# A mixture-of-experts tail with 26 units in place of 28: the largest experts in three strips of 32 slots, each beside a small expert

## The chip, the cores and the metric

The kernel runs on one core of a Trainium2 chip. A core has five engines: TensorE (PE, with its weight loads shown as PEld), VectorE (DVE), ScalarE (ACT), GpSimd (POOL) and SyncE (SP, here the engine that issues nearly all loads). Sixteen DMA engines move data between HBM and the on-chip SBUF. The metric is the device time of one execution in microseconds (us), the median over several runs.

## The reference

Two blocks run one after the other on 256 tokens of width 1024: a transformer block with two feed-forward layers, and a second block that ends in a mixture of experts. Only the end of the second block is touched here. In outline:

```
scores = sigmoid(h @ w_router)                  # 256 tokens x 64 experts
sel = scores + b_router; keep the best 4 of 8 groups of experts
top_e = top_k(sel, 8)                           # each token goes to 8 experts
w = scores[top_e] / sum * 2.5
for each expert e, on its own tokens:
    gate, up = split(h[tok] @ w_gu[e])          # w_gu[e]: 1024 x 512
    acc[tok] += w * ((silu(gate) * up) @ w_down[e])   # w_down[e]: 256 x 1024
y = acc + shared expert(h)                      # one expert that sees every token
out = x + gt2 * rms_norm(y)
```

All is float32. The experts' weights are 6144 numbers on each of 128 partitions, 3 MB for one expert and 192 MB for 64. Every expert's weights are read once. Counted from the reference for the given inputs, the 2048 pairs of token and expert spread unevenly: the largest expert has 73 tokens, the fifth largest 56, and the smallest 28 of the first 58 have 29 or fewer.

## The kernel before

Everything up to the router is the same instruction for instruction in both kernels and is left out here.

**Units.** The experts run in units of 128 slots. A slot is a place for one token of one expert. `UNITS` (line 33) is the order of the units, one letter each: F, two experts fixed by their number (the last eight, `NFIX`, "given" because no routing result is needed to know which they are); M, two experts of up to 64 tokens; H, one expert of up to 128 tokens; S, four experts of up to 32 tokens. Which experts take the places of H, M and S is found on the chip: `placement` (line 1616) ranks the first 56 experts by their count of tokens, so that the 4 largest fall to H, the next 28 to M, the rest to S. A list `plan` (line 1644) holds the expert's number for every place. Experts whose tokens don't fit would go through a loop at line 1911 that runs as often as needed; by the counts above it runs no time in either kernel.

**What a unit does on TensorE.** For each pair of units `gather` (L1792) picks the tokens' rows by a product with a one-hot matrix. Then, for each unit: `front` (L1809) multiplies the 128 slots by the gate and up weights in eight steps of 128 rows; each expert takes its own columns of the array (two of 64, one of 128, four of 32), and the first four steps read the expert's first tile, the last four its second. `back` (L1824 to L1846) transposes the activation, multiplies it by the down weights (L1841, the expert's third tile), scales by the routing weight on ACT and DVE. `scatter` (L1853) adds the result to the tokens' accumulators; it is issued one unit later, between the next unit's front and back.

**What orders the loads.** SP issues all expert loads (L1735) from one queue, in the order of the units, in tiles of 1 MB: in a unit first all first tiles, then all second, then all third, so an S unit has 12, F and M 6, H 3. There are 19 buffers (`NEX` + `NEX2`), used in turn: a load waits until TensorE has done the last product with the tile 19 places earlier. The numbers of a unit's experts are read from `plan` into SP's registers just ahead of that unit's loads (`entry`, L1741); the given experts need no such read. So SP can run ahead of TensorE by up to 19 tiles, but stops at the first planned unit until `plan` is written. In this text e1 to e192 are the expert tiles in the order of their loads; e1 to e24 belong to the four F units.

**Side work.** In the first units TensorE, DVE and ACT also do the shared expert, `placement` and `overflow`, in pieces between the expert products.

Of the kernel before, what the change touches and what calls it, by code (L numbers as in the profile page):

```python
# [13 lines left out]
ALU = mybir.AluOpType  # L14
# [6 lines left out]
T = 256  # L21
# [4 lines left out]
N_EX = 64  # L26
# [4 lines left out]
NFIX = 8  # L31
UNITS = "FFFFSSMHMSMMHMSMMHMSMMMHSMMM"
ROOM = {"F": (2, 64), "H": (1, 128), "M": (2, 64), "S": (4, 32)}
# [3 lines left out]
def column_plan():  # L37


    count = {k: UNITS.count(k) * ROOM[k][0] for k in "HMS"}  # L40
    assert sum(count.values()) == N_EX - NFIX and 2 * UNITS[:NFIX // 2].count("F") == NFIX
    at = {"H": 0, "M": count["H"], "S": count["H"] + count["M"]}
    cols, first = [], []
    for k in UNITS[NFIX // 2:]:
        first.append(len(cols))
        for _ in range(ROOM[k][0]):
            cols.extend((at[k], s) for s in range(0, ROOM[k][1], 64))
            at[k] += 1
    return cols, first, count["H"], count["H"] + count["M"]


COLS, FIRST_COL, RANK_M, RANK_S = column_plan()
NCOL = len(COLS)

# [94 lines left out]
class Kern:  # L149
# [55 lines left out]
    def root(self, v, b, n):  # L205

        nc = self.nc
        r = self.small([128, 1], "r", 12)
        nc.scalar.activation(r, v, AF.Sqrt, scale=1.0 / n, bias=b)  # L209
        nc.vector.reciprocal(r, r)  # L210
        return r
# [691 lines left out]
    def second_ffn(self, p):  # L903
# [11 lines left out]
        def load_x():  # L915
            for c in range(2):
                nc.gpsimd.dma_start(out=cx[:, c, :], in_=A["ctx"][128 * c:128 * c + 128, :])
            self.lower = self.small([128, 128], "lower", 1)
            nc.gpsimd.dma_start(out=self.lower, in_=A["lower"])
# [56 lines left out]
        inside = {}  # L976
# [70 lines left out]
        def root(c):  # L1047


            V = nc.vector  # L1050
            self.share(ss[c], 1024)
            t = self.small([128, 1], "r", 12)
# [354 lines left out]
    def post(self, ctx, ws_ctx):  # L1407
# [23 lines left out]
        self.at = self.small([128, 128], "lower", 1)  # L1431
# [184 lines left out]
    def placement(self):  # L1616
# [7 lines left out]
        ranks, bases = self.at[0:64, 0:NCOL], self.at[0:64, 64:64 + NCOL]  # L1624
# [22 lines left out]
        V.tensor_scalar(room, rank, RANK_M - 0.5, -64.0, op0=ALU.is_lt, op1=ALU.mult)  # L1647
# [71 lines left out]
    def load_unit(self, n):  # L1719

        u = n - NFIX // 2
        if u < 0:
            idx = [N_EX - NFIX + 2 * n + e for e in range(2)]
        else:
            idx = self.entry(self.plan, FIRST_COL[u], ROOM[UNITS[n]][0])
        self.ex[n] = [[] for _ in idx]
        yield from self.load_experts(idx, self.ex[n])
# [32 lines left out]
    def experts(self):  # L1760
# [40 lines left out]
        def front(ws, xg, j, inside={}):  # L1801

            r, o = 128 // len(ws), 128 * j
            gu = self.psw()
            for k in range(8):
                for f in inside.get(k, ()):
                    f()
                for e, w in enumerate(ws):
                    nc.tensor.matmul(gu[r * e:r * e + r, :], xg[:, k, o + r * e:o + r * e + r],  # L1809
                                     w[k // 4][:, 512 * (k % 4):512 * (k % 4) + 512], start=(k == 0), stop=(k == 7))  # L1810
            sil = self.small([128, 256], "sil", 1)
            nc.scalar.activation(sil, gu[:, 0:256], AF.Silu)  # L1812
            act = self.small([128, 256], "a32", 1)
            nc.vector.tensor_tensor(act, sil, gu[:, 256:512], op=ALU.mult)  # L1814
            return act

        def back(ws, act, ow, j, scatter=lambda c, nb: None):

            r = 128 // len(ws)
# [69 lines left out]
        for n in range(NUNIT):  # L1889
# [4 lines left out]
            act = front(ws, grp[0], n % 2, {} if n else {1: [lambda: next(self.shared)], 3: [lambda: next(side)],  # L1894
# [7 lines left out]
            pend = scatter(*back(ws, act, grp[1], n % 2, pend))  # L1902
# [8 lines left out]
        with tc.For_i(0, n, 2) as i:  # L1911
# [4 lines left out]
            all4(scatter(*back(ws, front(ws, grp[0], 0), grp[1], 0)))  # L1916
# [46 lines left out]
def _prepare(I):  # L1963
# [112 lines left out]
    at = np.zeros((128, 128), f32)  # L2076
    at[:, 0:NCOL] = [r for r, _ in COLS]
    at[:, 64:64 + NCOL] = [-s for _, s in COLS]
# [17 lines left out]
```

## Time and profile before

| | us |
|---|---|
| median of 3 runs | 1328.0 |
| lowest and highest | 1327.46, 1329.39 |
| the profiled execution | 1328.14 |
| its span | 1326.4 |
| PE busy | 1270.5 (96%) |
| DVE, ACT, POOL busy | 645.9, 525.6, 227.6 |
| DMA moved | 374.45 MB, mean 282 GB/s |
| first expert product (L1809) | 855.6 |
| last scatter (L1853) ends | 1316.1 |

The span runs from the first to the last instruction of the profile; the execution's own time is 1.7 us more. Matmuls are pipelined and their ends modelled, so a busy PE may still be waiting inside its rows. The 40 digits of the page's second part are slices of 33 us. The part that the change touches runs from about 855 to 1316 us.

### The profile page before, as it was taken

The numbers are of one execution on the slowest core, as the hardware profiler recorded it, in microseconds if no ns is written. First come the engines' busy times: TensorE is split into PE (matmuls) and PEld (weight loads), VectorE is DVE, ScalarE is ACT, GpSimd is POOL, SyncE is SP. The second block draws the span as 40 slices with busy tenths as digits, with TensorE's granted clock in tenths as the row PEclk, the third lists the DMA queues.
The fourth block names the chain that finished last, engine by engine and source line by source line (L and its number), as shares of the span: only waits on it lengthen the run. The fifth ranks groups of instructions, "written<-read, shape, count | busy, mean of one in ns | idle before, by whom it ended". The sixth has DMA issues, their size and how long they took to land. (4 is left out here: it accounts for less than half of the span.)

```text
span 1326.4 us, 20235 instructions
## 1 busy us (share of the span) xinstructions
PE 1270.5 (96%) x7812; PEld 923.4 (70%) x7812; DVE 645.9 (49%) x984; ACT 525.6 (40%) x883; POOL 227.6 (17%) x230
## 2 busy tenths in 40 slices
PE   7999999999999999989988899999999998999986
PEld 6889887988698998878887897544444443534532
DVE  5664555836657456676779546423222221212213
ACT  6534444557554456556644444311111111111112
POOL 1111112123023000125146442200000000000000
PEclk8999999999999999999999999999999999999999
DMA  7767678554385575646424378899999999999994
GB/s 303 252 232 280 248 279 304 157 169 163 120 331 189 189 254 180 219 174 244 144 96 143 129 287 323 340 379 373 400 420 420 420 420 419 421 420 420 420 420 190
DMA packets 72817, 374.45 MB, mean 282 GB/s; under 512 B 8932, under 2 KB 9364, under 8 KB 44304
## 3 DMA queue, kind: packets, MB, share of 16 engines
q1 hardware_dynamic: 68912, 361.25, 71.4%
q0 software_dynamic: 3664, 11.89, 2.6%
q8 instruction: 62, 1.02, 0.3%
q14 instruction: 35, 0.29, 0.1%
q10 hardware_dynamic: 144, 0.01, 0.0%
HBM read 371.99 MB, written 1.11 MB: 281 GB/s over the span
## 5 line engine op out<-in xcount | busy, mean ns | idle before, releaser
L137 DVE TENSOR_TENSOR wlo<-wland,whi 128x1024 fp32r<-128x1024 f32 x201 | 244.1, 1248 | 103.1 <-ACT whi L134 102.2
L258 PE MATMUL pw<-hT,whi 128*128 128x256 f32 x1856 | 250.4, 282 | 0.0
L134 ACT CAST whi<-wland 128x1024 fp32r<-128x1024 f32 x236 | 237.3, 1046 | 23.6 <-PE pa L267 12.7
L258 PEld LDWEIGHTS pw<-hT,whi 128*128 128x128 f32 x1856 | 232.8, 189 | 12.6 <-ACT whi L134 4.8
L1809 PE MATMUL pw<-ex,xg 128*64 128x512 f32 (+2 forms) x1024 | 205.2, 596 | 4.8 <-DMA ex<-ex 4.8
L1809 PEld LDWEIGHTS pw<-ex,xg 128*64 128x64 f32 (+2 forms) x1024 | 67.0, 130 | 128.7 <-issue 104.1
L258 PE MATMUL pw<-hT,wlo 128*128 128x256 f32 x928 | 128.2, 280 | 0.1
L1841 PE MATMUL pw<-ex,al 128*64 128x512 f32 (+2 forms) x512 | 112.2, 612 | 7.3 <-DMA ex<-ex 7.3
L258 PEld LDWEIGHTS pw<-hT,wlo 128*128 128x128 f32 x928 | 117.2, 189 | 0.3 <-POOL wlo L137 0.3
L137 POOL TENSOR_TENSOR wlo<-wland,whi 128x1024 fp32r<-128x1024 f32 x35 | 87.3, 2495 | 161.9 <-ACT whi L134 127.1
L267 PE MATMUL pa<-whi,hT 128*128 128x512 f32 x352 | 114.3, 400 | 0.0
L1814 DVE TENSOR_TENSOR a<-sil,pw 128x256 f32<-128x256 f32 x28 | 11.8, 421 | 189.0 <-ACT sil L1812 189.0
L1846 DVE SCALAR_TENSOR_TENSOR grow<-pw,sw,yh 128x512 fp32r<-128x512 f32 x56 | 42.1, 751 | 110.3 <-ACT yh L1845 109.4
L1812 ACT ACTIVATE sil<-pw 128x256 f32<-128x256 f32 x28 | 10.7, 384 | 207.6 <-PE pw L1809 207.6
L700 POOL TENSOR_TENSOR al<-a,ah 128x256 fp32r<-128x256 f32 x44 | 32.4, 736 | 330.0 <-ACT ah L699 329.9
L1841 PEld LDWEIGHTS pw<-ex,al 128*64 128x64 f32 (+2 forms) x512 | 31.7, 132 | 73.5 <-issue 49.6
L1845 ACT ACTIVATE yh<-pw,sw 128x512 fp32r<-128x512 f32 x56 | 38.5, 687 | 109.6 <-PE pw L1841 109.6
L1780 POOL TENSOR_TENSOR grow<-hx,Wp 128x256 f32<-128x256 f32 x24 | 14.6, 629 | 378.8 <-DVE hx L1778 378.8
L694 ACT ACTIVATE sil<-pw 128x256 f32<-128x256 f32 x44 | 16.9, 384 | 154.9 <-PE pw L258 154.8
L267 PEld LDWEIGHTS pa<-whi,hT 128*128 128x128 f32 x352 | 66.5, 189 | 16.1 <-DVE hT L248 0.4
L267 PE MATMUL pa<-wlo,hT 128*128 128x512 f32 x176 | 70.2, 399 | 5.1 <-DVE wlo L137 3.4
L267 PE MATMUL pa<-wlo,ah 128*128 128x512 f32 x176 | 69.7, 396 | 0.0
(404 smaller groups left out, 1781.8 us busy)
## 6 DMA issues: line engine op xcount, KB each, us to landing
ex<-ex SPq DMA_DIRECT2D x192, 1024.0 KB
wland<-wd SPq DMA_DIRECT2D x236, 512.0 KB
ada<-ada SPq DMA_DIRECT2D x24, 1024.0 KB
row<-rows POOLq DMA_DIRECT2D x6, 512.0 KB, 5.0
ex<-exs SPq DMA_DIRECT2D x3, 1024.0 KB
bias<-bscr POOLq DMA_DIRECT2D x4, 512.0 KB, 4.6
x<-x SPq DMA_DIRECT2D x4, 256.0 KB
pw<-poolw SPq DMA_DIRECT2D x2, 512.0 KB
```

The lines of the kernel that those rows point to most:

```text
L134: nc.scalar.copy(h, t)
L137: eng.tensor_tensor(l, t, h, op=ALU.subtract)
L258: self.nc.tensor.matmul(out, a[:, o:o + 128], b[:, k, :], start=(p == 0 and k == 0), stop=(p == 2 and k == nk - 1))
L267: self.nc.tensor.matmul(out, a[:, k, cs], b[:, lo:lo + n], start=(first and p == 0), stop=(last and p == 2))
L694: nc.scalar.activation(sil, ps[:, 0:256], AF.Silu)
L700: nc.gpsimd.tensor_tensor(al[:, 0, :], a, ah[:, 0, :], op=ALU.subtract)
L1780: nc.gpsimd.tensor_tensor(view(ow), view(oh), W[:, :, :, None].to_broadcast(shape), op=ALU.mult)
L1809: nc.tensor.matmul(gu[r * e:r * e + r, :], xg[:, k, o + r * e:o + r * e + r], w[k // 4][:, 512 * (k % 4):512 * (k % 4) + 512], start=(k == ...
L1814: nc.vector.tensor_tensor(act, sil, gu[:, 256:512], op=ALU.mult)
L1841: nc.tensor.matmul(y[r * e:r * e + r, :], aT[:, f, r * e:r * e + r], w[2][:, 1024 * f + 512 * nb:1024 * f + 512 * nb + 512], start=(f == 0 ...
L1845: nc.scalar.activation(yh[:, sl], y, AF.Copy, scale=sw)
L1846: nc.vector.scalar_tensor_tensor(yl[:, sl], y, sw, yh[:, sl], op0=ALU.mult, op1=ALU.subtract)
```

## The change

The units become 26. Two of the given experts (numbers 56 and 57) join those that are ranked, so that 58 are ranked and three F units are left, which shortens the given loads from 24 tiles to 18. The letter H goes. A new unit T holds one of the four largest experts (L, up to 96 slots in three strips of 32) and one small expert (a fourth strip of 32). M units fall from 14 to 13; S stays at 6; four T replace four H. The rooms are checked against the counts by the same overflow loop.

```
-NFIX = 8
-UNITS = "FFFFSSMHMSMMHMSMMHMSMMMHSMMM"
-ROOM = {"F": (2, 64), "H": (1, 128), "M": (2, 64), "S": (4, 32)}
+NFIX = 6
+UNITS = "FFFSSTMMSTMMSTMMSTMMSMMMMM"
+ROOM = {"F": 64, "L": 96, "M": 64, "S": 32}
+PARTS = {"F": "FF", "M": "MM", "T": "LS", "S": "SSSS"}
...
+def strips(unit):
+
+    at, out, n = 0, [], min(ROOM[k] for k in PARTS[unit])
+    for k in PARTS[unit]:
+        out.append([(at + s, n) for s in range(0, ROOM[k], n)])
+        at += ROOM[k]
+    return out
...
-        r = self.small([128, 1], "r", 12)
+        r = self.small([128, 1], "r", 8)
...
-        V.tensor_scalar(room, rank, RANK_M - 0.5, -64.0, op0=ALU.is_lt, op1=ALU.mult)
+        V.tensor_scalar(room, rank, RANK_M - 0.5, -32.0, op0=ALU.is_lt, op1=ALU.mult)
...
-            idx = self.entry(self.plan, FIRST_COL[u], ROOM[UNITS[n]][0])
+            idx = [x for c in OWN_COLS[u] for x in self.entry(self.plan, c, 1)]
...
-                for e, w in enumerate(ws):
-                    nc.tensor.matmul(gu[r * e:r * e + r, :], xg[:, k, o + r * e:o + r * e + r],
-                                     w[k // 4][:, 512 * (k % 4):512 * (k % 4) + 512], start=(k == 0), stop=(k == 7))
+                for w, own in zip(ws, strips(unit)):
+                    for s, r in own:
+                        nc.tensor.matmul(gu[s:s + r, :], xg[:, k, o + s:o + s + r],
+                                         w[k // 4][:, 512 * (k % 4):512 * (k % 4) + 512], start=(k == 0), stop=(k == 7))
...
-                    for e, w in enumerate(ws):
-                        nc.tensor.matmul(y[r * e:r * e + r, :], aT[:, f, r * e:r * e + r],
-                                         w[2][:, 1024 * f + 512 * nb:1024 * f + 512 * nb + 512],
-                                         start=(f == 0), stop=(f == 1))
+                    for w, own in zip(ws, strips(unit)):
+                        for s, r in own:
+                            nc.tensor.matmul(y[s:s + r, :], aT[:, f, s:s + r],
+                                             w[2][:, 1024 * f + 512 * nb:1024 * f + 512 * nb + 512],
+                                             start=(f == 0), stop=(f == 1))
```

The rest of the diff follows from this: the table of places grows from 60 to 66 columns (`colat`, 128 x 132 in place of 128 x 128), and the buffers of one-number tiles `r` fall from 12 to 8 to make room for it. Lines from 41 on stand 13 places or more later in the kernel after (L1735 is L1748, L1741 is L1754, L1809 is L1823, L1841 is L1855).

The first place where the order moves is SP's queue at the end of the given loads. Before (`ex_8616` is the last of the first 18 given tiles, `ex_8618` to `ex_8628` are those of the fourth F unit, `plan_8539` is the list of experts):

```order
L1735 DMA ex_8616<-ex 128x2048
L1735 DMA ex_8618<-ex 128x2048
L1735 DMA ex_8620<-ex 128x2048
L1735 DMA ex_8622<-ex 128x2048
L1735 DMA ex_8624<-ex 128x2048
L1735 DMA ex_8626<-ex 128x2048
L1735 DMA ex_8628<-ex 128x2048
L1741 TENSOR_LOAD plan_8539
```

And after, the same queue from the same tile on:

```order
L1748 DMA ex_8616<-ex 128x2048
L1754 TENSOR_LOAD plan_8539
L1754 ISA x2
L1754 TENSOR_LOAD plan_8539
L1754 ISA x2
L1754 TENSOR_LOAD plan_8539
L1754 ISA x2
L1754 TENSOR_LOAD plan_8539
L1754 ISA x2
L1748 ISA
L1748 DMA ex_8658<-ex 128x2048
```

The four reads of `plan` have moved ahead of six loads; what follows them is now the first tile of an S unit.

The second place is TensorE's front of a unit that holds one of the largest experts. Before, an H unit, all columns of the array for one expert (`ex_9069` and `ex_9197` are its first and second tile):

```order
L1841 MATMUL pw_9502<-ex2_9055,al_9482 64x512
L1841 MATMUL pw_9502<-ex_9057,al_9482 64x512
L1809 MATMUL pw_9541<-ex_9069,xg_9411 128x512 x4
L1809 MATMUL pw_9541<-ex_9197,xg_9411 128x512 x4
L1853 MATMUL pa_8510<-yh_9493,ah_9490 128x512
```

After, a T unit (`ex_8834` and `ex_8967` are the large expert's first and second tile, `ex_8965` and `ex2_8969` the small one's; two of the four steps on each tile are shown):

```order
L1823 MATMUL pw_9347<-ex_8834,xg_9177 32x512 x3
L1823 MATMUL pw_9347<-ex_8965,xg_9177 32x512
L1823 MATMUL pw_9347<-ex_8834,xg_9177 32x512 x3
L1823 MATMUL pw_9347<-ex_8965,xg_9177 32x512
...
L1823 MATMUL pw_9347<-ex_8967,xg_9177 32x512 x3
L1823 MATMUL pw_9347<-ex2_8969,xg_9177 32x512
```

One product of 128 columns has become four of 32, three of them with the same weights, and the unit reads two experts' tiles where it read one's.

## Rows read from the trace of the kernel before

**Rows 1.** Page, parts 1 and 2: TensorE's busy time, and GB/s by slice.
```profile
PE 1270.5 (96%) x7812; PEld 923.4 (70%) x7812; DVE 645.9 (49%) x984; ACT 525.6 (40%) x883; POOL 227.6 (17%) x230
GB/s 303 252 232 280 248 279 304 157 169 163 120 331 189 189 254 180 219 174 244 144 96 143 129 287 323 340 379 373 400 420 420 420 420 419 421 420 420 420 420 190
```

**Rows 2.** Windows: stretch, length, busy of PE/PEld/DVE/ACT/POOL, PEclk, DMA share, GB/s.
```profile
842.00:862.00 20.00, 20.00 (x96) 11.31 (x96) 9.84 (x53) 3.45 (x8) 1.76 (x3) 1.00 0.79 289
862.00:882.00 20.00, 20.00 (x86) 7.92 (x85) 4.15 (x15) 2.78 (x6) 0.00 (x0) 1.00 0.94 366
882.00:902.00 20.00, 20.00 (x109) 10.34 (x106) 4.98 (x11) 3.52 (x7) 1.29 (x2) 1.00 0.91 356
902.00:922.00 20.00, 19.45 (x102) 8.86 (x103) 7.57 (x27) 3.19 (x8) 1.22 (x2) 1.00 1.00 388
922.00:942.00 20.00, 20.00 (x162) 9.92 (x162) 4.95 (x9) 4.58 (x9) 0.00 (x0) 1.00 0.96 389
...
1042.00:1142.00 100.00, 96.51 (x474) 45.97 (x471) 22.36 (x43) 16.68 (x31) 3.64 (x6) 1.00 1.01 420
...
862.00:867.00 5.00, 5.00 (x24) 2.21 (x23) 1.99 (x11) 1.04 (x3) 0.00 (x0) 1.00 0.94 390
...
872.00:877.00 5.00, 5.00 (x20) 2.65 (x22) 0.94 (x2) 1.05 (x2) 0.00 (x0) 1.00 0.82 298
```

**Rows 3.** What SP's queue waited for, 841 to 932: total, times, longest.
```profile
SPq L1735 <- PE pw L1809: 30.4, 7, 8.3
```

**Rows 4.** The same view, 940 to 1290.
```profile
SPq L1735 <- DMA ex<-ex: 243.5, 134, 3.0
SPq L1735 <- PE pw L1841: 5.2, 9, 2.9
```

**Rows 5.** TensorE's timeline, an S unit: start, length, instruction, [idle before].
```profile
1001.38 7.24 PE L1809 MATMUL pw<-ex,xg 128*32 128x512 f32 x64
...
1011.06 1.05 PE L1841 MATMUL pw<-ex,al 128*32 128x512 f32 x4
...
1014.95 3.62 PE L1841 MATMUL pw<-ex,al 128*32 128x512 f32 x26 [1.45 <-DMA ex<-ex]
```

**Rows 6.** Lines by form, 760 to 1327: front products in three widths.
```profile
L1809 PE MATMUL pw<-ex,xg 128*64 128x512 f32 x576 | 131.6, 596 | 3.4 <-DMA ex<-ex 3.4
L1809 PE MATMUL pw<-ex,xg 128*32 128x512 f32 x384 | 45.1, 594 | 1.5 <-DMA ex<-ex 1.5
L1809 PE MATMUL pw<-ex,xg 128*128 128x512 f32 x64 | 28.4, 597 | 0.0
```

**Rows 7.** TensorE's timeline, the last two units (both M).
```profile
1283.48 4.15 PE L1792 MATMUL pt<-hx,h 128*128 128x256 f32 x32
1287.57 7.09 PE L1809 MATMUL pw<-ex,xg 128*64 128x512 f32 x32
...
1300.66 7.09 PE L1809 MATMUL pw<-ex,xg 128*64 128x512 f32 x32
```

**Rows 8.** VectorE's timeline: the list of experts is written.
```profile
862.35 0.21 DVE L1644 CAST plan<-pt 1x60 int32<-1x60 f32 x1 [1.50 <-PE pt L1642]
```

**Rows 9.** SP's timeline in three stretches, then its register work from 855 to 880.
```profile
860.44 4.57 SPq L1735 DMA_DIRECT2D ex<-ex  x4
...
872.00 0.80 SPq L1735 DMA_DIRECT2D ex<-ex  x2
...
876.89 3.92 SPq L1735 DMA_DIRECT2D ex<-ex  x2
...
L1735 SPq FUSED_REGOPS  x2: 42/45/48, 875.4 to 877.3; - x2
```

**Rows 10.** Windows and TensorE's timeline around an S unit where the clock fell.
```profile
1176.00:1180.00 4.00, 2.99 (x13) 0.80 (x11) 0.84 (x3) 0.37 (x1) 1.13 (x2) 1.00 1.01 422
1180.00:1184.00 4.00, 3.17 (x16) 0.80 (x20) 0.00 (x0) 0.00 (x0) 0.00 (x0) 0.61 1.02 424
...
1180.83 5.31 PE L1841 MATMUL pw<-ex,al 128*32 128x512 f32 x26 [1.45 <-DMA ex<-ex]
```

More of the change, by code (lines that the diff above doesn't have):

```diff
@@ L30 @@
 NEX2 = 8
-NFIX = 8
-UNITS = "FFFFSSMHMSMMHMSMMHMSMMMHSMMM"
-ROOM = {"F": (2, 64), "H": (1, 128), "M": (2, 64), "S": (4, 32)}
+NFIX = 6
+UNITS = "FFFSSTMMSTMMSTMMSTMMSMMMMM"
+ROOM = {"F": 64, "L": 96, "M": 64, "S": 32}
+PARTS = {"F": "FF", "M": "MM", "T": "LS", "S": "SSSS"}
 NUNIT = len(UNITS)
 def column_plan():
[L40 to L44, printed above, removed]
+    count = {k: sum(PARTS[u].count(k) for u in UNITS) for k in "FLMS"}
+    assert UNITS[:NFIX // 2] == "F" * (NFIX // 2) and count["F"] == NFIX and sum(count.values()) == N_EX
+    at = {"L": 0, "M": count["L"], "S": count["L"] + count["M"]}
+    cols, first, own = [], [], []
+    for u in UNITS[NFIX // 2:]:
         first.append(len(cols))
-        for _ in range(ROOM[k][0]):
-            cols.extend((at[k], s) for s in range(0, ROOM[k][1], 64))
+        own.append([])
+        for k in PARTS[u]:
+            own[-1].append(len(cols))
+            cols.extend((at[k], s) for s in range(0, ROOM[k], 64 if u == "M" else 32))
             at[k] += 1
-    return cols, first, count["H"], count["H"] + count["M"]
-COLS, FIRST_COL, RANK_M, RANK_S = column_plan()
+    return cols, first, own, count["L"], count["L"] + count["M"]
+def strips(unit):
[4 more added lines that the diff above has]
+    return out
+COLS, FIRST_COL, OWN_COLS, RANK_M, RANK_S = column_plan()
 NCOL = len(COLS)
@@ L917, in load_x @@
                 nc.gpsimd.dma_start(out=cx[:, c, :], in_=A["ctx"][128 * c:128 * c + 128, :])
-            self.lower = self.small([128, 128], "lower", 1)
+            self.lower = self.small([128, 2 * NCOL], "lower", 1)[:, 0:128]
             nc.gpsimd.dma_start(out=self.lower, in_=A["lower"])
@@ L1051, in root @@
             self.share(ss[c], 1024)
-            t = self.small([128, 1], "r", 12)
+            t = self.small([128, 1], "r", 8)
             V.tensor_scalar(t, ss[c][:, 1:2], 1.0 / 1024, ss[c][:, 0:1], op0=ALU.mult, op1=ALU.add)
@@ L1430, in post @@
         nc.gpsimd.dma_start(out=self.ei, in_=self.A["eidx"])
-        self.at = self.small([128, 128], "lower", 1)
+        self.at = self.small([128, 2 * NCOL], "lower", 1)
         nc.gpsimd.dma_start(out=self.at, in_=self.A["colat"])
@@ L1623, in placement @@
         idx, given, key0 = ei[:, 0:1], ei[:, 2:3], ei[:, 3:4]
-        ranks, bases = self.at[0:64, 0:NCOL], self.at[0:64, 64:64 + NCOL]
+        ranks, bases = self.at[0:64, 0:NCOL], self.at[0:64, NCOL:2 * NCOL]
         n = N_EX - NFIX
@@ L1799, in gather, with front @@
             return xg, ow
-        def front(ws, xg, j, inside={}):
-            r, o = 128 // len(ws), 128 * j
+        def front(ws, unit, xg, j, inside={}):
+            o = 128 * j
             gu = self.psw()
@@ L1815, in front, with back @@
             return act
-        def back(ws, act, ow, j, scatter=lambda c, nb: None):
-            r = 128 // len(ws)
+        def back(ws, unit, act, ow, j, scatter=lambda c, nb: None):
             for c, nb in ((0, 0), (0, 1), (1, 0)):
@@ L1893, in experts @@
                 grp = gather(*oh, 2)
-            act = front(ws, grp[0], n % 2, {} if n else {1: [lambda: next(self.shared)], 3: [lambda: next(side)],
+            act = front(ws, UNITS[n], grp[0], n % 2, {} if n else {1: [lambda: next(self.shared)], 3: [lambda: next(side)],
                                                            6: [lambda: next(side)]})
@@ L1901, in experts @@
                 oh = onehot(two(n + 1))
-            pend = scatter(*back(ws, act, grp[1], n % 2, pend))
+            pend = scatter(*back(ws, UNITS[n], act, grp[1], n % 2, pend))
             next(side, None)
@@ L1915, in experts @@
             grp = gather(*onehot([(self.slotx[:, :, ds(i, 2)], self.Wx[:, :, ds(i, 2)])]), 1)
-            all4(scatter(*back(ws, front(ws, grp[0], 0), grp[1], 0)))
+            all4(scatter(*back(ws, "M", front(ws, "M", grp[0], 0), grp[1], 0)))
         self.warm(AF.Sqrt)
@@ L2075, in _prepare @@
     ei[:, 3] = -ei[:, 0] - 1.0e6 * (1.0 - ei[:, 2])
-    at = np.zeros((128, 128), f32)
+    at = np.zeros((128, 2 * NCOL), f32)
     at[:, 0:NCOL] = [r for r, _ in COLS]
-    at[:, 64:64 + NCOL] = [-s for _, s in COLS]
+    at[:, NCOL:] = [-s for _, s in COLS]
     A["colat"] = at
```

## The prediction

> **What bounds the kernel now.** I read the page first. TensorE is busy 96% of the span, but the last row of GB/s stands at 420 in slice after slice from about 930 us on [rows 1]. A flat rate that no engine's pattern marks is the sign of a stream that runs at its own limit, whatever the busy share of TensorE says. So I cut the expert stage into windows. Between 842 and 942 us the DMA engines move 289, 366, 356, 388 and 389 GB/s; from then on 420, with a busy share of 1.01 [rows 2]. Who holds the loads back shows in what SP's queue waited for: in the early stretch it is TensorE (a buffer not yet free), 30.4 us in the largest group alone; from 940 on it is an earlier DMA, 243.5 us in 134 waits, against 5.2 us for the largest wait on TensorE [rows 3, 4]. In the late stretch a faster TensorE makes nothing arrive sooner.
>
> One tile is 128 x 2048 x 4 bytes, 1.0486 MB; at 420 GB/s it takes 2.50 us. All 192 take 479.4 us, and neither kernel loads one tile more or less.
>
> TensorE's own pace is close to that. In the last two units the gather starts at 1283.48, the fronts at 1287.57 and 1300.66 [rows 7]: a unit is 13.09 us, the gather that two units share 4.09, so a pair costs 30.27 us. The 12 tiles of two M units take 29.96. TensorE is thus 0.31 us slower than the DMA in every pair of M units. In an S unit it is the other way round: 12 tiles for one unit, and TensorE waits (in the S unit at 1001 the back begins at 1011.06 but its large block only at 1014.95 [rows 5]).
>
> **The change, part by part.**
>
> *Two units less on TensorE.* 28 units are 14 pairs, 14 x 30.27 = 423.8 us; 26 are 393.5. The 30.3 us saved are off the path wherever the 420 stand: they become waits of TensorE on expert tiles. I count them as nothing after 942 us.
>
> *T in place of H.* A front took 131.6 us in 18 units of two 64-column experts, 45.1 in 6 of four of 32, 28.4 in 4 of one of 128 [rows 6] (a unit has 32, 64 or 16 records): 7.31, 7.52 and 7.10 us, the first two with 3.4 and 1.5 us of idle inside the groups. The width makes no difference, so a T front costs 7.1 as H's did, if its strips run side by side. Three strips with the same weights are not in the trace. The bounds are no extra cost (as in S) and three strips one after the other: two more fronts of 7.1 and two more backs of 3.6 (the large block of [rows 5]), 21.4 us a T unit. The groups STMM have 30 tiles, 74.9 us, and 2 pairs, 60.5 us, on TensorE; with 21.4 they would need 81.9 and set the pace by 7.0, four times, +28 us. I take no extra cost: the nearest row is S, whose four strips differ from these only in whose weights they read. H had three tiles for the same TensorE time, so T evens out the demand, which changes who waits, not when the last tile lands.
>
> *Six given experts.* Here the order moves something that is on the path. The list of experts is written at 862.56 us (862.35 + 0.21) [rows 8]. SP issued e19 to e22 from 860.44 on, e23 and e24 at 872.00, finished at 872.80, and had its first planned register at 875.4 [rows 9], with the list long written: four reads cost 2.6 us. In the kernel after, e19 is itself planned. It can issue at 862.56 + 2.6 + 0.2 = 865.4, where it stood at 860.44: 4.9 us later. Nothing else is queued behind these reads on SP but expert loads, all of them. Taken alone this moves the whole stream by 4.9 us.
>
> *What the stream gets back.* Before, 842 to 862 is bound by the router's end and is the same in both. From 862 to 942 the DMA moved (366 + 356 + 388 + 389) x 20 = 29.98 MB [rows 2] of the 33.60 that 420 GB/s allow: 8.6 us were lost, to buffers that TensorE had not freed. After, the stream lies still until e19 flows, 4.9 us later than before, and to that comes what 862 to 867 lost before (390 GB/s, 0.4 us). But now six tiles are asked for nearly at once, 15 us of work, and the ring's next buffers come free at the same times as before, since the first three units are unchanged: e23 and e24 at 872.0, when the DMA has work until about 878 (before, it ran dry here: 298 GB/s at 872 to 877 [rows 2]); e25 at 876.9, e26 and e27 by 880.8 [rows 9]. The frees in the third F unit come one unit and one gather, 17.2 us, after those in the second: e32 at about 898, e36 (the back's end) at 908 to 909, e38 (the next front's half) at 911 to 913. With tile k done at about 867.5 + 2.50 (k - 18), e32 is asked for two tiles ahead of its turn, e36 and e38 just at theirs: at most 0.8 us of gaps. From e38 on the buffers come from the S unit that now stands fourth. It frees four tiles with every half of its front, 3.5 us, where a fourth F unit freed two. So from about 915 the stream is full, some 25 us sooner than before. Lost after: 4.9 + 0.4 + 0.8 = 6.1. Against 8.6 the DMA gains 2.5 us. The ends: nothing regained, +4.9 (every later gap as before); all regained, -8.6. I take -2.3, a little under the walk's sum, since the frees in the third unit may come late by some side work; both ends are kept for the range.
>
> *The tail.* After the last S unit TensorE sets the pace at 0.31 us a pair over the DMA. Before, three M units follow it, after, five: one pair more, +0.3.
>
> *Waits that grow.* TensorE has 30 us more to wait, in S units above all. The row that shows what that can do: at 1180 to 1184 the granted clock is 0.61, so for most of it at the lower level, 1.2 GHz, after a stretch in which TensorE was busy 2.99 of 4 us; the back's large block took 5.31 there [rows 10] against 3.62 in the S unit at 1014.95 [rows 5]. One fall costs 1.7 us of TensorE. In the middle the next wait absorbs it. The M unit behind the last S unit must wait too, since its six tiles, 15.0 us, land only after the S unit's last and TensorE needs 13.09 for them, so a fall in that S unit is mostly absorbed as well; what falls later is not. I add 0.2. Bounds: 0 (all absorbed) and 3.4 (two falls, none absorbed).
>
> The Trainium skill, "TensorE: Matmul & The Clock Gate", section "HAM oscillation — how this bites in real kernels", says that a kernel whose TensorE waits on DMA between short blocks pays the clock's warm-up each time. This trace shows it once (1.7 us, above). By that rule each S unit with a long wait after would start its work cold, and the sum would change only by what the last of them passes on: rival 4.
>
> *The rest.* 66 places for 60 in a dozen small DVE and PE steps, 2 KB more in `colat`, 8 `r` buffers in place of 12 whose readers are far behind: the steps are of some 0.2 us [rows 8] and grow by a tenth. Bounds 0 and +0.3 us on the way to the list; I take 0.
>
> Sum: -2.3 + 0.3 + 0.2 = -1.8 us on the profiled execution's 1328.14 (span 1326.4 and 1.74 around it): 1326.3. That execution is 0.14 above the median of the runs, so I say 1326.3 as the median too, rounded within their spread of 1.9.
>
> **Rivals.**
>
> 1. *TensorE sets the end.* Then two units less are worth 30.3 us: 1297.8. For it: 96% busy [rows 1]. Against it: 420 GB/s flat for 360 us and SP waiting on DMA [rows 2, 4]. Chance 0.03.
>
> 2. *The early loss goes for the most part.* Three F units and an S unit free the ring faster than I walk, the reads of the list cost less, and the DMA runs at 420 from about 864 on: between -3 and -8.3 (8.6 less the tail), middle 1323. For it: the S unit stands one place earlier, and the 8.6 us are there. Against it: the list's 862.56 is fixed by the same instructions as before. Chance 0.16.
>
> 3. *The reads of the list hold the stream and nothing makes up for it (the slower side).* The place is SP's queue between e18 and e19, the price +4.9, with the tail 1333.3. It decides once the gaps between 882 and 942 regain less than 2 us, that is, if TensorE's frees in the third F unit are as late for the stream as they were. For it: 356 GB/s at 882 to 902 [rows 2], no better than at 862 to 882, so the ring was short of buffers there for another reason than the list. Against it: at 865 four buffers stand free, and two more come before the DMA is through with those. Chance 0.10. (That the strips of T run one after the other, +28, has 0.02 beside it.)
>
> 4. *The clock falls in the tail*: one or two falls unabsorbed after the last S unit, +1.7 to +3.4 less the DMA's 2.0: 1328 to 1329.6. For it: a group STMM leaves TensorE 14.4 us idle (74.9 - 60.5), most of it in the S unit, where the one at 1001 waited 3.9 [rows 5]. Against it: the stretch from 1042 to 1142, with an S unit in it, has a granted clock of 1.00 [rows 2]. Chance 0.09.
>
> **How the numbers follow.** My forecast, the DMA-bound end with small terms, has 0.60. What a measurement of this kernel can tell from no change is 0.2%, 2.65 us, so 1325.3 to 1330.7. The forecast of -1.8 lies inside it, with perhaps a sixth of its chance below 1325.3: 0.10 faster, 0.50 same. Rival 1 and 2 add 0.19 to faster; rival 4 0.08 to same and 0.01 to slower; rival 3, with the strips, 0.12 to slower. Faster 0.29, same 0.58, slower 0.13. The forecast's own range is 1324.7 to 1328.2. For 8 in 10 it must take in half of rival 2 and most of rival 4, and leave out rivals 1 and 3 for the most part: 1323.6 to 1330.0.
>
> **What would show it.** Right: GB/s of 420 from about 920 on in place of 942; less than the 390 of before at 862 to 867, then 420 at 872 to 877, where before it dipped; SP's first planned register near 865; TensorE's waits on expert tiles up by some 30 us; the last scatter near 1314. Wrong: gaps in the 420 later than 940 (buffers held by T units would do that, if a T front took 21 us), a first planned load later than 867, or a T front unlike 7.1 us. The prediction as a whole fails if the last tile lands more than 4 us earlier or at all later than before.

## The result: 8 us slower, nearly all of it before the changed stage

The kernel after takes 1336.5 us (median of 6 runs, 1334.1 to 1338.4) against 1328.7 for the kernel before (6 runs, 1327.5 to 1331.1): a ratio of 1.0053, 95% interval 1.0039 to 1.0067. The forecast was 1326.3, its range 1323.6 to 1330.0. The profiled execution of after took 1338.41 us, 10.3 more than that of before; it is the slowest of its six.

The first question for a trace like this is where the difference begins. Both kernels run the same instructions up to the experts, so one asks each line for its first and last start (the two numbers behind the durations' minimum, median and maximum). Before, the feed-forward's 256-column products and the experts' front products:

```profile
L258 PE MATMUL pw<-hT,whi x1856: 274/280/683, 31.8 to 779.5; 128*128 128x256 f32 x186
L1809 PE MATMUL pw<-ex,xg x1024: 592/592/697, 855.6 to 1307.2; 128*64 128x512 f32 x97, 128*32 128x512 f32 x64, 128*128 128x512 f32 x10
```

After (the lines have moved by 13 and 14):

```profile
L271 PE MATMUL pw<-hT,whi x1856: 274/281/683, 32.1 to 788.0; 128*128 128x256 f32 x186
L1823 PE MATMUL pw<-ex,xg x1152: 592/592/1063, 864.8 to 1317.4; 128*32 128x512 f32 x106, 128*64 128x512 f32 x86
```

The same 1856 products take 755.9 us from first to last in place of 747.7. The first expert product, with which the changed part begins, starts 9.2 us late, at 864.8. From there to the last front it is 452.6 us against 451.6. So the stage that I forecast is 1 us longer, and 9 us are lost where both kernels run the same instructions, with buffers at other addresses.

The loss is no wait. Four windows cut the first part; the first one, before and then after (columns as in [rows 2]):

```profile
40.00:240.00 200.00, 199.55 (x1424) 173.77 (x1423) 113.24 (x136) 88.54 (x127) 28.97 (x42) 1.00 0.73 263
```

```profile
40.00:240.00 200.00, 199.57 (x1398) 173.93 (x1398) 110.86 (x135) 86.89 (x126) 29.22 (x43) 1.00 0.73 261
```

TensorE is as busy (199.6 us) at the same granted clock of 1.00, but in these 200 us it starts 1398 products in place of 1424. The single product has become slower. Its duration in the trace hides that (280 and 281 ns at the median: neighbours overlap and the ends are modelled); the pace is the time from the start of one product to the start of the next. In the timeline, before and then after, one pass over hT in each:

```profile
162.20 1.10 PE L258 MATMUL pw<-hT,whi 128*128 128x256 f32 x8
163.14 1.10 PE L258 MATMUL pw<-hT,wlo 128*128 128x256 f32 x8
164.07 2.03 PE L258 MATMUL pw<-hT,whi 128*128 128x256 f32 x16
165.94 1.10 PE L258 MATMUL pw<-hT,wlo 128*128 128x256 f32 x8
```

```profile
164.67 1.12 PE L271 MATMUL pw<-hT,whi 128*128 128x256 f32 x8
165.63 1.12 PE L271 MATMUL pw<-hT,wlo 128*128 128x256 f32 x8
166.59 2.08 PE L271 MATMUL pw<-hT,whi 128*128 128x256 f32 x16
168.51 1.12 PE L271 MATMUL pw<-hT,wlo 128*128 128x256 f32 x8
```

Sixteen products take 165.94 - 164.07 = 1.87 us before, 116.9 ns each, and 1.92 us after, 120 ns each. (The moving operand of a product is the one that streams past the weights; here it is hT, the activations.) Over all consecutive records whose moving operand is hT the mean step is 116.85 ns before and 119.92 after. There are 2880 such products: 2880 x 3.07 = 8.8 us of the 9.2.

What differs is where the operands lie. The program's list of allocations shows it: 8 `r` buffers in place of 12 take 128 bytes (32 each) from the pool, so hT moves from byte 37568 to 37440 of each partition; the larger tables (`lower`, `plan`, `slotp`, `Wp`) give 192 back, so everything behind the pool, the weight buffers among them, moves from 65440 to 65504. In what follows the **distance** is the address of the moving operand less that of the weights loaded next, modulo 512 bytes. Both advance in multiples of 512, so one number holds for all products of hT by 256 columns in the feed-forward: 288 before, 96 after. For the same reason it is also the distance to a product's own weights, and no run here tells the two apart.

The stage itself went by most steps of the prediction. Page of after, then its windows with the limits moved on by 9 us (the first five are a stretch of 20, 20, 20, 20 and 100 us from 871 on, the last two the counterparts of 862 to 867 and 872 to 877):

```profile
PE 1269.0 (95%) x7948; PEld 912.3 (68%) x7948; DVE 638.5 (48%) x970; ACT 520.2 (39%) x873; POOL 226.8 (17%) x228
GB/s 301 246 231 272 247 268 302 159 170 174 112 325 197 190 247 167 208 184 253 131 112 126 127 275 327 354 323 398 419 419 419 419 420 419 420 419 419 419 419 173
```

```profile
871.00:891.00 20.00, 20.00 (x84) 7.92 (x84) 4.17 (x15) 2.78 (x6) 0.00 (x0) 1.00 0.76 304
891.00:911.00 20.00, 20.00 (x110) 10.11 (x104) 4.99 (x11) 3.31 (x6) 1.29 (x2) 1.00 1.01 414
911.00:931.00 20.00, 19.45 (x146) 8.82 (x150) 7.58 (x27) 3.26 (x7) 1.23 (x2) 1.00 0.99 388
931.00:951.00 20.00, 20.00 (x167) 9.80 (x162) 4.95 (x9) 4.41 (x9) 0.00 (x0) 1.00 1.02 420
951.00:1051.00 100.00, 94.42 (x596) 41.45 (x590) 21.48 (x41) 15.69 (x30) 3.71 (x6) 1.00 1.01 419
...
871.00:876.00 5.00, 5.00 (x23) 2.16 (x22) 1.71 (x11) 0.89 (x3) 0.00 (x0) 1.00 0.01 3
...
881.00:886.00 5.00, 5.00 (x20) 2.54 (x18) 1.02 (x3) 1.05 (x2) 0.00 (x0) 1.00 1.02 431
```

Against [rows 2]: the stream lies still where it had 390 GB/s, runs at 431 where it had 298, and is full from 931 on, that is 922 on the clock of before, in place of 942. The list of experts, SP's wait for it (its end is put down to a later VectorE step, 0.5 us behind the list's) and SP's register work ([rows 8, 9]):

```profile
871.64 0.22 DVE L1657 CAST plan<-pt 1x66 int32<-1x66 f32 x1 [1.50 <-PE pt L1655]
```

```profile
SPq L1754 <- DVE hx L1663: 11.0, 1, 11.0
```

```profile
L1748 SPq FUSED_REGOPS  x8: 37/46/51, 874.8 to 886.6; - x8
```

The list is written at 871.86 and the first planned register read at 874.8, 10.0 us behind the first expert product; forecast was 865.4 - 855.55 = 9.9. The front of an S unit and, below it, the first one of a T unit; then the weight loads' waits on expert tiles, in before (from 929 us on) and in after:

```profile
937.00 7.07 PE L1823 MATMUL pw<-ex,xg 128*32 128x512 f32 x64
950.62 7.07 PE L1823 MATMUL pw<-ex,xg 128*32 128x512 f32 x64
```

```profile
PEld pw L1841 <- DMA ex<-ex: 14.5, 8, 2.4
PEld pw L1809 <- DMA ex<-ex: 11.3, 10, 2.4
```

```profile
PEld pw L1823 <- DMA ex<-ex: 44.1, 28, 2.9
PEld pw L1855 <- DMA ex<-ex: 8.8, 5, 2.4
```

The T front takes 7.07 us like the S front. The waits are 52.9 us against 25.8: a growth of 27.1 where 30 were forecast. The clock fell in these waits more often than before. Windows around one case:

```profile
1076.00:1080.00 4.00, 2.30 (x4) 0.14 (x2) 0.00 (x0) 0.00 (x0) 0.00 (x0) 0.83 1.00 410
1080.00:1084.00 4.00, 3.17 (x16) 0.79 (x20) 0.00 (x0) 0.00 (x0) 0.00 (x0) 0.50 1.03 426
```

In the second stretch the granted clock is the lower level, 1.2 GHz, after one in which TensorE was busy 2.30 of 4 us. It happened four times in the stage (at 1078, 1153, 1228 and 1252 us), once before (at 1181, [rows 10]).

### The profile page after: what moved, and what is told of

Read it like the earlier page. It is cut to its first block, busy times and chain, and to the rows that moved or that the text cites. A ratio compares the mean times of both kernels' runs of the same rounds, so it can differ in the third digit from the quotient of the medians.

```text
span 1336.6 us, 20485 instructions
## 1 busy us (share of the span) xinstructions
PE 1269.0 (95%) x7948; PEld 912.3 (68%) x7948; DVE 638.5 (48%) x970; ACT 520.2 (39%) x873; POOL 226.8 (17%) x228
## 5 line engine op out<-in xcount | busy, mean ns | idle before, releaser
L271 PE MATMUL pw<-hT,whi 128*128 128x256 f32 x1856 | 255.0, 284 | 0.0
L271 PEld LDWEIGHTS pw<-hT,whi 128*128 128x128 f32 x1856 | 237.3, 189 | 12.3 <-ACT whi L147 4.8
L1823 PE MATMUL pw<-ex,xg 128*32 128x512 f32 (+1 forms) x1152 | 212.7, 625 | 20.6 <-DMA ex<-ex 20.4
L1823 PEld LDWEIGHTS pw<-ex,xg 128*32 128x32 f32 (+1 forms) x1152 | 59.0, 126 | 160.3 <-issue 105.5
L271 PE MATMUL pw<-hT,wlo 128*128 128x256 f32 x928 | 131.0, 283 | 0.0
L271 PEld LDWEIGHTS pw<-hT,wlo 128*128 128x128 f32 x928 | 119.9, 189 | 0.0
L1828 DVE TENSOR_TENSOR a<-sil,pw 128x256 f32<-128x256 f32 x26 | 10.9, 421 | 213.2 <-ACT sil L1826 213.2
L1855 PE MATMUL pw<-ex,al 128*32 128x512 f32 (+1 forms) x576 | 100.1, 597 | 4.3 <-DMA ex<-ex 4.3
L1860 DVE SCALAR_TENSOR_TENSOR grow<-pw,sw,yh 128x512 fp32r<-128x512 f32 x52 | 39.0, 750 | 96.4 <-ACT yh L1859 96.4
L1859 ACT ACTIVATE yh<-pw,sw 128x512 fp32r<-128x512 f32 x52 | 35.8, 688 | 95.7 <-PE pw L1855 95.7
L1855 PEld LDWEIGHTS pw<-ex,al 128*32 128x32 f32 (+1 forms) x576 | 26.9, 121 | 64.0 <-issue 46.5
```

The costliest lines, as they stand in the source:

```text
L271: self.nc.tensor.matmul(out, a[:, o:o + 128], b[:, k, :], start=(p == 0 and k == 0), stop=(p == 2 and k == nk - 1))
L1823: nc.tensor.matmul(gu[s:s + r, :], xg[:, k, o + s:o + s + r], w[k // 4][:, 512 * (k % 4):512 * (k % 4) + 512], start=(k == 0), stop=(k == 7))
L1855: nc.tensor.matmul(y[s:s + r, :], aT[:, f, s:s + r], w[2][:, 1024 * f + 512 * nb:1024 * f + 512 * nb + 512], start=(f == 0), stop=(f == 1))
```

## Experiments

Two theories stood at the start: the early 9 us come from the operands' places, or from the program (its order, its length, the larger table loads). Runs a and b tell them apart; c, d and f ask whether one operand's place or the distance counts.

**a: the kernel before with the addresses of after.**

```diff
-        r = self.small([128, 1], "r", 12)
+        r = self.small([128, 1], "r", 8)
-            self.lower = self.small([128, 128], "lower", 1)
+            self.lower = self.small([128, 132], "lower", 1)[:, 0:128]
-        self.plan = self.small([1, NCOL], "plan", 1, I32)
+        self.plan = self.small([1, 66], "plan", 1, I32)[:, 0:NCOL]
(slotp and Wp likewise at 66 columns; where r or lower is allocated a second time, the same edit, left out here and below)
```

> The kernel before, its 28 units and its order untouched, with every SBUF tile at the address that it has in the kernel after: 8 `r` buffers in place of 12, which pulls hT, h2 and sil 128 bytes down, and tables padded to 66 columns, which push the weight buffers wland, whi, wlo and the expert stage's xg, h2T, fo 64 bytes up. Theory 1 (addresses): the 9 us that the kernel after lost ahead of its first expert product come from the pace of the feed-forward's matmuls, which depends on where the two operands lie; then this kernel shows them too, with the first expert product near 864 in place of 855.6 and a time of 1335 to 1338. Theory 2 (the program: its order, its longer or shorter instruction stream, the table loads of another size): the early loss goes with the units, so this kernel stays at 1327 to 1330 with the first expert product near 855.5.

1337.9 us, ratio to before 1.0060 (1.0041 to 1.0079). Its row:

```profile
L1809 PE MATMUL pw<-ex,xg x1024: 592/592/697, 864.7 to 1316.6; 128*64 128x512 f32 x97, 128*32 128x512 f32 x64, 128*128 128x512 f32 x10
```

First expert product at 864.7, mean step 119.91 ns: the whole loss, without one unit changed.

**b: the kernel after with the addresses of before.**

```diff
-        r = self.small([128, 1], "r", 8)
+        r = self.small([128, 1], "r", 12)
-        self.ei = self.small([64, 4], "ei", 1)
+        self.ei = self.small([64, 28], "ei", 1)[:, 0:4]
-        self.plan = self.small([1, NCOL], "plan", 1, I32)
+        self.plan = self.at[0:1, 0:NCOL].bitcast(I32)
```

> The kernel after, its 26 units and its order untouched, with the large tiles (hT, h2, sil, the weight buffers, xg, h2T, fo) at the addresses of the kernel before: 12 `r` buffers again, the plan kept in a part of the table tile that is free by then, and 96 bytes of padding behind `ei`. Theory 1 (addresses): the early loss goes, first expert product at 855 to 857, and 470.9 to 471.8 us of expert stage behind it give 1327 to 1330, the time of the kernel before. Theory 2 (the program): 1335 to 1338 as the kernel after. What remains against the kernel before in this run is the price of the units alone: my prediction had -1.8 us for it, the stage's length in the two traces says +1.

1328.8 us, ratio 0.9991 (0.9981 to 1.0000). By the ratio the units alone are thus worth -1.2 us (-2.5 to 0); the forecast for them was -1.8. Its rows:

```profile
L1823 PE MATMUL pw<-ex,xg x1152: 592/592/1062, 855.8 to 1306.3; 128*32 128x512 f32 x106, 128*64 128x512 f32 x86
```

```profile
862.00:882.00 20.00, 20.00 (x84) 7.92 (x84) 4.17 (x15) 2.79 (x6) 0.00 (x0) 1.00 0.76 304
882.00:902.00 20.00, 20.00 (x108) 10.12 (x104) 4.99 (x11) 3.31 (x6) 1.30 (x2) 1.00 1.01 415
902.00:922.00 20.00, 19.45 (x146) 8.75 (x148) 7.58 (x27) 3.25 (x7) 1.22 (x2) 1.00 0.99 394
922.00:942.00 20.00, 20.00 (x166) 9.78 (x162) 4.95 (x9) 4.47 (x9) 0.00 (x0) 1.00 1.01 419
```

The fronts span 450.5 us, 1.1 less than before. Between 862 and 942 the DMA moved (304 + 415 + 394 + 419) x 20 = 30.64 MB against 29.98: at 420 GB/s 1.6 us gained, with the standstill at the list already paid.

**c and d: one operand alone.** c has hT 128 bytes lower (8 `r` buffers, the gap filled behind the table), d the weights 64 bytes higher (padding behind the table, 12 `r` buffers).

```diff
-            self.lower = self.small([128, 128], "lower", 1)
+            self.lower = self.small([128, 160], "lower", 1)[:, 0:128]     # c, with "r" at 8
+            self.lower = self.small([128, 144], "lower", 1)[:, 0:128]     # d, with "r" at 12
```

> The kernel before with 8 `r` buffers and 128 bytes of padding behind the table: hT, h2 and sil lie 128 bytes lower as in the kernel after, the weight buffers stay. Theory 1a (the place of the moving operand hT by itself, or against the weights): part or all of the 9 us, first expert product at 860 to 865. Theory 1b (only the weight buffers' place counts): 855.5 and 1328. A rival within: the four `r` buffers less bring waits of their own; then this kernel is slow too, but in the norms, not in the feed-forward's matmuls.

> The kernel before with 12 `r` buffers and 64 bytes of padding behind the table: the weight buffers (wland, whi, wlo) and the expert stage's xg, h2T, fo lie 64 bytes higher as in the kernel after, hT and h2 stay. Theory 1b (the weight buffers' place): 1335 to 1338, the first expert product near 864. Theory 1a (hT's place by itself): 1328. If both tiles' distance counts, c and d each show some other pace of the 256-column matmuls than the kernels before (117 to 119.5 ns from start to start) and after (120.7 to 122 ns).

c: 1331.0 us, ratio 1.0011 (1.0000 to 1.0022), first expert product at 856.1. d: 1332.6, ratio 1.0024 (1.0015 to 1.0034), 859.5. Neither gives the 9 us, and the delays of the first expert product, 0.6 and 3.9 us, don't add up to the 9.1 of a: the two places don't act each for itself. (The paces that the expectation of d gives are rough readings; the means are 116.85 before and 119.92 after.) c has 8 `r` buffers, so waits for the missing four cost at most what c shows, 0.2%.

**f: both moved alike.** Only `r` goes from 12 to 10.

> The kernel before with 10 `r` buffers in place of 12 and nothing else: hT, h2 and the weight buffers all move 64 bytes down, so that their distance stays (moving operand minus weights = 288 bytes, modulo 512) while each address changes as much as one of them did in d. Theory 1c (only the distance of a matmul's two operands counts): the hT products keep 116 to 117.5 ns from start to start, first expert product at 855 to 857, time 1327 to 1330 (the tiles at fixed places, ex and hq, change their distance to the weights and may cost or give some tenths). Theory 1d (the address of a tile by itself counts, modulo 128 or so): a pace like that of d or of the kernel after, first expert product at 859 to 865, 1332 to 1338.

1328.2 us, ratio 0.9996 (0.9985 to 1.0008), first expert product at 855.5, mean step 116.80 ns. hT and the weights have both moved by 64 bytes and nothing has changed, while the 64 bytes of d, for the weights alone, cost 3.4 us. What counts is the distance.

**g: the pace by itself.**

```diff
+            for k in range(n):
+                a = mo // 4 + cols * (k % 8)
+                w = wo // 4 + 128 * (k % 8)
+                nc.tensor.matmul(out[:, 0:cols], wgt[:, w:w + 128], mov[:, a:a + cols], start=True, stop=True)
```

> Leaves out the whole computation: it loads x, makes of it a moving operand and a row of weights in SBUF, and runs groups of 24 float32r matmuls, 128 partitions by 256 columns with 128 columns of weights, each with its own weights, as the feed-forward does (moving operand 1024 bytes further and weights 512 bytes further from product to product). The groups differ in the place of the two operands alone: weights 0, 32, ... 480 bytes further, for the moving operand at 0, 32, 64 and 96 bytes; some with the weights 512 bytes further still; and 16 groups of 512 columns. TensorE does nothing else and no transfer runs. Theory 1c (the distance counts, modulo 512 bytes): the mean step of a group depends on the distance alone, within 0.5 ns for the four places of the moving operand; slow at a distance of 0 and 96 (120 ns), quick at 64, 160, 288 and 320 (117 ns), as in the traces of the whole kernels, and a distance of 512 is one of 0. Theory 1d (a single address): the groups line up by the weights' place or by the moving operand's, not by their difference. Rival (transfers or other engines that write SBUF at the same time set the pace): all groups have one step, within 1 ns.

Rows of its timeline (a group's name holds the bytes by which the moving operand and the weights are set off; its 24 steps are the difference to the next row's start):

```profile
29.59 3.04 PE L1983 MATMUL a0x0x<-mov,wgt 128*128 128x256 f32 x24
32.47 3.00 PE L1983 MATMUL a0x32x<-mov,wgt 128*128 128x256 f32 x24
35.30 2.99 PE L1983 MATMUL a0x64x<-mov,wgt 128*128 128x256 f32 x24
38.13 2.98 PE L1983 MATMUL a0x96x<-mov,wgt 128*128 128x256 f32 x24
...
80.72 3.05 PE L1983 MATMUL a64x64x<-mov,wgt 128*128 128x256 f32 x24
83.60 3.00 PE L1983 MATMUL a64x96x<-mov,wgt 128*128 128x256 f32 x24
86.44 2.91 PE L1983 MATMUL a64x128x<-mov,wgt 128*128 128x256 f32 x24
89.18 3.04 PE L1983 MATMUL a64x160x<-mov,wgt 128*128 128x256 f32 x24
...
259.73 2.90 PE L1983 MATMUL r0x64x<-mov,wgt 128*128 128x256 f32 x24
262.46 3.00 PE L1983 MATMUL r0x32x<-mov,wgt 128*128 128x256 f32 x24
```

a0x0x and a64x64x, both at distance 0, take 2.88 us, 120 ns a product; a64x128x, at 448, takes 2.74, 114.2 ns. The mean steps of all groups, sorted by distance (the four places of the moving operand and the repeated series; 448 stands with 192 and so on, since the pairs that differ by 256 agree, save for single groups at 160 and 192):

```
distance mod 256          0          32         64         96         128        160        192        224
256 columns, ns   119.5-120.2 116.7-117.9 117.7-118.0 119.5-120.1 118.3-118.9 117.2-120.1 113.9-117.8 118.1-118.4
512 columns, ns   226.6-229.1    233.4       229.8       233.6       231.7       233.5       233.5       232.9
```

The theory of the distance holds for most of the table, and with nothing else running, so neither transfers nor other engines make it: at 0, 64, 96, 128 and 224 the groups of one distance lie within 0.7 ns, wherever the moving operand lies. Two points of the expectation were off. The pattern repeats after 256 bytes, not 512. And for 32, 160 and 192 there is more than one pace, which a group keeps to its last product (in a64x128x single steps of 113 and 114 ns from the fourth on). There the distance doesn't decide alone, nor do the addresses: a0x64x and r0x64x have the very same two places and take 117.8 and 113.9 ns. What chooses between the paces is open.

**h, j, k: a distance chosen from this table.** The 512-column products have the roles changed (the weight stream moves, hT is loaded as weights), so their distance is the negative.

```diff
-        r = self.small([128, 1], "r", 12)
+        r = self.small([128, 1], "r", 9)                                  # h: hT 96 bytes lower
-            self.lower = self.small([128, 128], "lower", 1)
+            self.lower = self.small([128, 152], "lower", 1)[:, 0:128]     # h: the weights stay
(j: weights 160 bytes lower, plan in the table as in b; k: "r" at 11, table 32 bytes longer)
```

> The kernel before with 9 `r` buffers and 96 bytes of padding behind the table: hT and h2 lie 96 bytes lower, so that moving operand minus weights is 192 bytes (modulo 512) in place of 288; the weight buffers stay. By run g's groups a 256-column product at 192 takes 113.9 ns or 117.8 ns (two paces, one for a whole group) and the 512-column products, where the roles are changed, 229.8 in place of 232.9 to 233.4. With about 2650 products of hT by 256 columns (116.8 ns now) and 850 by 512: between -10 and 0 us, so 1318 to 1329, first expert product at 845 to 855.5. Rival (the slow or quick pace of g doesn't carry over to a program with transfers and other engines beside): 1328, or slower by the 3 us of an arbitrary distance.

> The kernel before with the weight buffers 160 bytes lower and hT where it is: distance 448. If distances count modulo 256 bytes, as the pairs of g that differ by 256 say, it has the pace of h (192): the same time within 2 us. If a distance counts modulo 512, 448 is another case: 113.9 or 117.8 for the 256 columns by g, too, but not in step with h.

> The kernel before with 11 `r` buffers and 32 bytes of padding behind the table, so that hT and h2 alone move, by 32 bytes: distance 256. By g a 256-column product takes 119.6 to 120 ns there (116.8 now) and a 512-column one 226.6 to 229.1 (232.9 now): 2650 times +3 ns and 850 times -5 ns make +3 to +5 us, the first expert product at 858.5 to 860.5, 1331 to 1334. If only the 256-column products counted: +8 us, 1336. Rival (32 bytes are too little to count): 1328.

h: 1318.5 us, ratio 0.9921 (0.9903 to 0.9938). j: 1318.4, ratio 0.9921 (0.9903 to 0.9938). k: 1332.1, ratio 1.0027 (1.0017 to 1.0037). The timeline of h, one pass as above:

```profile
159.77 1.09 PE L258 MATMUL pw<-hT,whi 128*128 128x256 f32 x8
160.70 1.07 PE L258 MATMUL pw<-hT,wlo 128*128 128x256 f32 x8
161.61 1.98 PE L258 MATMUL pw<-hT,whi 128*128 128x256 f32 x16
163.42 1.07 PE L258 MATMUL pw<-hT,wlo 128*128 128x256 f32 x8
```

Sixteen products in 1.81 us, 113.1 ns each. The whole kernels, mean steps from consecutive records:

```
kernel        distance   256 columns   512 columns   first expert product   median
k                256        119.86        228.7            860.5            1332.1
after, a          96        119.9         233.9        864.8, 864.7    1336.5, 1337.9
c                160        117.67        233.9            856.1            1331.0
d                224        118.33        233.4            859.5            1332.6
before, b, f     288        116.8         233.3        855.6, 855.8, 855.5  1328.7, 1328.8, 1328.2
j                448        114.85        229.7            847.9            1318.4
h                192        114.41        229.3            846.5            1318.5
```

Worked out from these, h has 2880 x 2.44 + 990 x 3.9 = 10.9 us to gain over before (the 990 are the 512-column steps that could be read) and gains 9.1 up to the first expert product; k has 2880 x 3.0 - 990 x 4.6 = +4.1 and shows +4.9. c is the poorest fit: +3.0 by the table, +0.6 at the first expert product; its profiled execution, 1328.4 us, was the fastest of its ten, 2.6 under their median.

**i: the units of after at distance 192.** b with `r` at 9 and 96 bytes more of padding.

> The kernel of b (the units after, large tiles where the kernel before has them) with 9 `r` buffers and 96 bytes of padding more, distance 192. If h gains x, this gains the same x on b's 1328.8, since the units act behind the first expert product only: 1318 to 1329. If the expert stage is bound by its transfers from its first product on, no part of x is lost there.

1319.2 us, ratio 0.9929 (0.9912 to 0.9945). Its fronts span 450.2 us against 451.4 in h. The gain of the distance comes through in full; whether the units add to it can't be told, the intervals of h and i overlap. h, i and j beat both kernels.

**e: eight given experts in the new plan.**

```diff
-NFIX = 6
+NFIX = 8
-UNITS = "FFFSSTMMSTMMSTMMSTMMSMMMMM"
+UNITS = "FFFFSSTMMSTMMSTMMSTMMSMMMM"
(against the kernel after; the large tiles at the addresses of before, as in b)
```

> The units after, but with eight given experts in place of six (one F pair more, one M pair less; 26 units still), the large tiles at the addresses of the kernel before. It tests the one step of the forecast that spoke against the change: with six, the first load that needs the plan (expert tile 19) is issued 10.2 us after the first expert product, with eight it should go out 5 us after it as in the kernel before. Theory A (the transfers set the end, so an early gap comes through): 4 to 5 us faster than b (1328.8), 1323 to 1325. Theory B (the stream makes the gap good, since buffers come free at TensorE's pace later on, or the gap only moves to the first load that does need the plan): 1328 to 1329, the same as b.

1329.4 us, ratio 1.0000 (0.9988 to 1.0011). Its 19th expert load, which needs no plan here, is issued at 861.9, 4.9 us behind the first expert product; in b, where it does, it is 866.0, 10.2 us behind. The two windows in which b gained:

```profile
882.00:902.00 20.00, 20.00 (x108) 10.25 (x106) 4.99 (x11) 3.31 (x6) 1.29 (x2) 1.00 0.89 343
902.00:922.00 20.00, 19.45 (x104) 8.99 (x102) 7.58 (x27) 3.25 (x7) 1.22 (x2) 1.00 0.99 388
```

343 GB/s where b has 415: the stream starts sooner and then lacks free buffers again, as before (from 882 to 902 SP waits 17.6 us for the front's and the back's expert products in e, 12.2 in b). Theory A fails, theory B holds: the standstill at the list and the S unit that stands a place earlier come out even. No run changes one of the two without the other, so what each is worth alone is not shown.

## Why the prediction was wrong

**The step that failed** is the term called "The rest": "8 `r` buffers in place of 12 whose readers are far behind", taken as 0 with bounds 0 and +0.3 us. Run a measures that edit, with the padding that the 66 columns bring: +8.0 us by the ratio (8.7 between the medians), of which waits for the missing buffers are at most 0.2% of the time (c). I had asked of each buffer only who waits for it, not what lies behind it in the pool. No row of the trace of before gave a price for a matmul at another address, and I did not name the place of the operands as an unknown; so the upper bound of 0.3 had no ground. The chance of "slower" (0.13) was made of rivals 3 and 4 and the strips, and none of them happened.

**What held.** The end is bound by the transfers: two units less make no 30 us, and 27 us of TensorE's time became waits on tiles. T costs what S and H cost: its front takes 7.07 us (H 7.10 by [rows 6]), so the +28 of serial strips did not come. The first planned register came 10.0 us after the first expert product (forecast 9.9), and the stream was full some 20 us sooner (forecast 25). The net of the early stretch was -1.6 in b against -2.3. One reading there was too simple: the 8.6 us lost before were all put down to buffers that TensorE had not freed, but 1.5 of them lie at 902 to 922, where the DMA share is 1.00 in [rows 2], and 394 GB/s in b against 388 show that hardly any of this came back. Rival 3, the standstill with nothing to make up for it, had about the right price for the standstill (the 19th load goes out at 866.0 in b, at 860.4 before) and is refuted by b, which is 1.2 us quicker than before where this rival has 5.2 slower. Rival 1 (-30 us) is refuted by b: at equal addresses the two units less, and all that comes with them, are worth 1.2 us. Rival 2 did not come: 304 GB/s at 862 to 882 in b, not 420. So the sum stood for the units: b's 1328.8 lies in the range of the forecast.

**Clock falls.** The forecast gave them 0.2 us. The Trainium skill, "TensorE: Matmul & The Clock Gate", section "HAM oscillation — how this bites in real kernels", says that waits on transfers between short blocks of products make the clock fall again and again. The traces agree on the direction: one fall became four in after and in b, and two in e and in i, though these kernels have ten units of four strips (S and T). The falls cost nothing that shows at the end: b has granted clocks of 0.98, 0.97 and 0.95 in the windows of 100 us from 942 on, where before has 1.00, 1.00 and 0.98, and its fronts still span 1.1 us less.

**What is left in the stage of after itself** is 452.6 us of fronts against 451.9 in a, at equal addresses, and 450.5 in b. Its stream ran at 419 GB/s in place of 420 ([rows 1]), about 0.8 us over 350; for the rest one profile of each kernel can't tell cause from chance.

## What to carry to other kernels

An edit that changes the size or count of any buffer moves what is allocated behind it, and on a kernel bound by TensorE's small matmuls that alone was worth -10 to +9 us here, more than the edit's own effect. So compare the addresses of the large operands before and after, and when they differ, pad until they agree and time the edit again; then treat the distance between moving operand and weights as a setting of its own. Read the pace of pipelined matmuls from start to start, or from how many of the same products fit in a fully busy window, not from their durations.

## What the runs showed of the hardware

In run g a product of 256 columns in float32r, the type of these operands in the kernel, with new weights each time, took from 113.9 to 120.2 ns at the full clock, by the distance of its two operands in SBUF and, at 32, 160 and 192, by something more that stays open. The pattern repeats every 256 bytes, and 512-column products vary from 226.6 to 233.6 ns by another pattern. Moving both operands alike made no difference in f, and within 0.7 ns none in g at the other distances.

The Trainium skill, "SBUF — State Buffer", section "SBUF: two separate sides", says that on the engines' side only the port pair shared by VectorE and GpSimd causes contention and that TensorE never waits on anyone. Run g doesn't speak against that, for no other engine works there; but TensorE's pace still changes by 5% with the weights' place, so a TensorE that waits on no other engine need not run at one pace. How the two places act on the pace, no run here shows.

The same skill, "TensorE: Matmul & The Clock Gate", section "Back-to-back issue gap", gives 262 cycles for 256 columns as the gap of a product without the budget of a weight load; at 2.4 GHz that is an estimate of 109 ns. The quickest pace measured here, with a weight load for each product, is 4% above it, the slowest 10%.
